# Half of an input projection by a seven-product scheme, in a phase of its own, with its results kept in DRAM

## The chip, the cores and the metric

The kernel runs on one core of one Trainium2 chip. The metric is the time of one execution on the device in microseconds (us), lower is better. The profile comes from one execution that the hardware profiler recorded. TensorE is called PE here, its weight loads PEld, VectorE DVE, ScalarE ACT, GpSimd POOL, and SyncE, which issues all DMAs of this kernel, SP.

## The reference

Two layers work on 1024 tokens of width 1024, float32 throughout. Each layer normalizes its input to h, projects it with one matrix of 1024 x 7764, runs three branches on parts of the result, gates and merges them:

```
p   = split_proj(h @ w_in[l])                    # 7764 columns
ret = rms_norm(retention(ret_q, ret_k, ret_v)) * silu(ret_g)
dsa = dsa_attention(...) * silu(dsa_g)           # top 256 keys per query
gl  = rms_norm(gla(gla_q, gla_k, gla_v, log_a)) * silu(gla_g)
g   = sigmoid(merge)                             # 3 x 1024 columns
y   = (g[0] * (ret @ w_br_ret) + g[1] * (dsa @ w_br_dsa) + g[2] * (gl @ w_br_gla)) @ w_out
x   = x + gate * rms_norm(y, post_norm)
```

## The kernel before

Every dense product is split in three: both operands are kept as a rounded high part and the low rest, and `mm3` (L222) issues high x high, low x high and high x low into the same PSUM bank. h lies transposed in SBUF as `hTh` and `hTl` (128 partitions, 8 blocks of the width, 1024 tokens). A projection comes in two forms. `nat` (L227) puts 128 tokens on the partitions and up to 512 output columns on the free axis, 24 matmuls for a block of tokens; `trans` (L235) puts 128 output columns on the partitions and 512 tokens on the free axis, 24 matmuls as well. Weights are loaded by `wload` or `wide` (L165, L207): one DMA of 256 KB, a cast on ACT for the high part (L176), a subtraction on POOL for the low part (L177). Three raw buffers and ten of each part rotate.

A layer goes in this order: index projection and index scores (`idx_proj`, `idx_scores`, L468 to L509); the retention with its V projection, its q and k projection, a scan over eight blocks and the gate (`ret_gate`, L609), which projects the gate columns, multiplies and transposes; the first GLA projection and scan (`gla_proj` L648, `gla_scan` L694); the merge of the retention (`merge`, L302), which projects 256 gate columns at a time, takes tanh, multiplies them with the branch product and stores the result in DRAM; the second GLA projection and scan, between whose blocks pieces of the conditioning of later norms are put (`cond_part`, L315, twelve in layer 0, four in layer 1); the GLA gates and the DSA gate (`gla_gate` L788, L811 to L818); the transposes of the GLA output and the merge of GLA; the top-k of the index scores (`topk`, L851), 32 rounds of an eight-fold maximum and a replacement for each block of 128 queries; the DSA projections, the attention, and with it the sixteen gate tiles of the DSA merge; the combination of the three branches (L1040 to L1056), the output projection, the norm and the next h.

The order of the instructions on each engine isn't written out: a scheduler lists them by the order of the program and puts later instructions forward where an engine would be idle by its own estimates and buffers are free. So the top-k of blocks 2 to 5 lies on DVE beside the retention and the first scan, and that of blocks 6 and 7 has an explicit edge behind the first product of the GLA merge (L860). Memory is a stack of pools on a left and a right side; a tile can be written when the tiles that lay there before are no longer read. The pools of the second GLA projection lie where the retention's output and the first merge lay.

A scan handles eight blocks of 128 tokens. For two blocks at a time, six levels of exponent tiles are made (L712 to L718: two subtractions on DVE, one exponential on ACT, three products on POOL); for each block then follow a transpose (L737), the state (L747, L753), six score matmuls (L762), seven masked copies on DVE (L763, L768), the output (L774, L778) and its sums of squares.

## Time and profile before

| | us |
|---|---|
| median of 3 runs | 2485.9 (2485.63 to 2487.37) |
| the profiled execution | 2489.89 |
| its span, first to last instruction | 2488.1 |
| busy: PE / PEld / DVE | 2395.1 / 2032.5 / 1704.3 |
| busy: ACT / POOL | 892.9 / 915.0 |

A line of a group of instructions has the line in the kernel, engine, operation, the tile that is written and those that are read, shapes, the count, then busy time and mean duration of one, then the idle time of the engine just before them with what ended it. A matmul's record runs from its issue to its modelled end, and records overlap. A line of stages has the two bounds and the length in us, then for each engine its busy time and count, the granted clock of TensorE as a share of 2.4 GHz, the busy share of the DMA engines and GB/s.

### The profile page before, as it was taken

What the parts mean: (1) busy time and instruction counts of PE and PEld (TensorE: products, weight loads), DVE (VectorE), ACT (ScalarE), POOL (GpSimd) and SP (SyncE); (2) the same over time, 40 slices, a digit from 0 to 9 for tenths busy, and PEclk for the clock granted to TensorE, in tenths of its full rate; (3) what the DMA queues carried; (4) which work ended last, traced back from release to release, by engine and by line L of the source; (5) the groups of instructions that cost most, each with busy time, mean ns of one, the idle gap of its engine ahead of it and who ended that gap; (6) DMA issues with size and microseconds to landing.
All of it is one profiled execution on the core that took longest, in us unless ns stands there. A gap on an engine that the chain in (4) does not pass through costs nothing.

```text
span 2488.1 us, 38048 instructions
## 1 busy us (share of the span) xinstructions
PE 2395.1 (96%) x13680; PEld 2032.5 (82%) x13680; DVE 1704.3 (68%) x3513; ACT 892.9 (36%) x2147; POOL 915.0 (37%) x1304
## 2 busy tenths in 40 slices
PE   8898999999999999999999899999999999999998
PEld 4777788888878998887788677887898789888777
DVE  6599997348749964567567999933554899356652
ACT  4333432232321236663433234222333212566421
POOL 4324344534522352106641244443454225310350
PEclk9999999999999999999999899999999999999999
DMA  8011112224412212007620111222321221210453
GB/s 273 22 35 35 35 41 79 59 87 145 119 60 76 66 48 64 27 22 246 201 90 1 35 35 48 64 61 85 85 63 41 85 85 35 71 41 22 140 199 110
DMA packets 153115, 194.95 MB, mean 78 GB/s; under 512 B 18703, under 2 KB 109147, under 8 KB 152926
## 3 DMA queue, kind: packets, MB, share of 16 engines
q1 hardware_dynamic: 152926, 192.52, 25.4%
q8 instruction: 107, 1.75, 0.3%
q14 instruction: 82, 0.67, 0.1%
HBM read 154.71 MB, written 37.77 MB: 77 GB/s over the span
## 4 chain that ended last, share of the span: by engine, by line
PE 73%; DVE 15%; DMA 4%; issue 3%; POOL 3%; ACT 2%; SPq 0%; DVEq 0%; POOLq 0%; ACTq 0%
PE acc L223 18%; PE acc L224 18%; PE acc L225 18%; DVE mk L855 3%; PE tp L936 2%; DVE m L854 2%; DMA craw<-in_ada_w 2%; PE sc L762 2%; PE o L958 1%; PE sc L921 1%; PE o L955 1%; PE sc L922 1%; PE o L962 1%; PE sc L223 1%; PE sc L224 1%
## 5 line engine op out<-in xcount | busy, mean ns | idle before, releaser
L223 PE MATMUL acc<-whi,hTh 128*128 128x256 f32 (+1 forms) x1600 | 509.8, 319 | 15.5 <-DVE rb L544 8.0
L225 PE MATMUL acc<-whi,hTl 128*128 128x256 f32 (+1 forms) x1600 | 507.4, 317 | 0.0
L224 PE MATMUL acc<-wlo,hTh 128*128 128x256 f32 (+1 forms) x1600 | 506.9, 317 | 0.0
L177 POOL TENSOR_TENSOR wlo<-raw,whi 128x512 fp32r<-128x512 f32 x216 | 283.1, 1318 | 374.8 <-ACT whi L176 343.6
L223 PE MATMUL acc<-hTh,whi 128*128 128x512 f32 x896 | 355.4, 397 | 2.7 <-ACT mt L287 1.8
L224 PE MATMUL acc<-hTl,whi 128*128 128x512 f32 x896 | 353.3, 394 | 0.0
L225 PE MATMUL acc<-hTh,wlo 128*128 128x512 f32 x896 | 352.7, 394 | 0.0
L854 DVE MAX8 m<-mk 128x8 f32<-128x512 f32 (+5 forms) x384 | 341.7, 892 | 8.2
L223 PEld LDWEIGHTS acc<-whi,hTh 128*128 128x128 f32 x1600 | 307.1, 192 | 41.3 <-issue 11.7
L855 DVE MATCH_REPLACE8 mk<-m,mk 128x512 f32<-128x512 f32 (+5 forms) x384 | 336.6, 877 | 0.2
L225 PEld LDWEIGHTS acc<-whi,hTl 128*128 128x128 f32 x1600 | 306.8, 192 | 20.0 <-issue 2.4
L224 PEld LDWEIGHTS acc<-wlo,hTh 128*128 128x128 f32 x1600 | 307.0, 192 | 19.0 <-issue 2.2
L176 ACT CAST whi<-raw 128x512 fp32r<-128x512 f32 x216 | 133.8, 622 | 217.9 <-PE acc L224 139.0
L223 PEld LDWEIGHTS acc<-hTh,whi 128*128 128x128 f32 x896 | 169.0, 189 | 39.9 <-ACT mt L287 2.8
L225 PEld LDWEIGHTS acc<-hTh,wlo 128*128 128x128 f32 x896 | 169.0, 189 | 37.1 <-issue 2.4
L224 PEld LDWEIGHTS acc<-hTl,whi 128*128 128x128 f32 x896 | 169.1, 189 | 34.1 <-issue 1.9
L940 DVE TENSOR_TENSOR ptl<-tp,pth 128x512 fp32r<-128x512 f32 (+1 forms) x160 | 100.6, 635 | 68.6 <-ACT pth L939 59.3
L287 ACT ACTIVATE mt<-acc 128x512 f32<-128x512 f32 x96 | 57.2, 599 | 191.1 <-PE acc L225 136.3
L218 POOL TENSOR_TENSOR wlo<-raw,whi 128x512 fp32r<-128x512 f32 x56 | 76.7, 1378 | 111.2 <-ACT whi L217 110.4
L926 ACT ACTIVATE P<-P,mx 128x256 f32<-128x256 f32 (+7 forms) x128 | 99.8, 781 | 47.0 <-DVE mx L923 46.1
L939 ACT CAST pth<-tp 128x512 fp32r<-128x512 f32 (+1 forms) x160 | 85.7, 545 | 69.5 <-PE o L955 43.3
L973 POOL TENSOR_TENSOR qo<-qo,gt 128x256 f32<-128x256 f32 x32 | 23.5, 735 | 229.4 <-DVE qo L967 208.8
(411 smaller groups left out, 4858.4 us busy)
## 6 DMA issues: line engine op xcount, KB each, us to landing
raw<-in_w_in SPq DMA_DIRECT2D x224, 256.0 KB
yscr<-mu SPq DMA_DIRECT2D x64, 256.0 KB
craw<-in_ada_w SPq DMA_DIRECT2D x64, 256.0 KB
ul<-yscr SPq DMA_DIRECT2D x64, 256.0 KB
aw<-in_ada_w SPq DMA_DIRECT2D x16, 512.0 KB
xt<-in_x SPq DMA_DIRECT2D x16, 512.0 KB
mscr<-mt SPq DMA_DIRECT2D x32, 256.0 KB
ul<-mscr SPq DMA_DIRECT2D x32, 256.0 KB
```

The costliest lines, as they stand in the source:

```text
L176: A.copy(hi[:, :, :off], raw[:, :, :off])
L177: G.tensor_sub(lo[:, :, :off], raw[:, :, :off], hi[:, :, :off].bitcast(FT))
L218: G.tensor_sub(lo, raw, hi.bitcast(FT))
L223: T.matmul(ps, ah, bh, start=start, stop=False)
L224: T.matmul(ps, ah, bl, start=False, stop=False)
L225: T.matmul(ps, al, bh, start=False, stop=stop)
L287: A.activation(t, gp, AF.Tanh, scale=0.5)
L854: V.max(m8, mk[i])
L855: V.match_replace(mk[i], m8, mk[i], TAKEN)
L926: A.activation(P[:, :N], P[:, :N], AF.Exp, scale=-1.0, bias=mx[:, nch - 1:nch], accum_out=den[:, i, n * 4 + g:n * 4 + g + 1])
L939: A.copy(pth[:, :w], tp[:, :w])
L940: V.tensor_sub(ptl[:, :w], tp[:, :w], pth[:, :w].bitcast(FT))
```

## The change

3584 of the 7764 columns (retention gate, GLA q and k, GLA gate, merge gates of the retention and of GLA) are computed in a function of their own, `dense`, right after the index scores, by Strassen's scheme in Winograd's form: the two halves of the 1024 input rows, two blocks of 128 columns and the two halves of the tokens make a 2 x 2 product, for which seven half-size products of 12 matmuls each take the place of eight. Sums of quarters of h (`Th`, `Tl`, four of each) are made once a layer; sums of quarters of the weights are made for each of the 14 groups of 256 columns; partial results are copied out of PSUM and added. All results are transposed (columns on partitions) and go to DRAM: tanh or SiLU already taken for gates. The merges load gate tiles instead of projecting them; the merge of GLA also adds the stored merge of the retention, so that the combination after attention loads one tensor less. The gates of retention and GLA are loaded and multiplied after the transposes of the branch outputs (`to_br`); before, they were multiplied ahead of the transposes. GLA q and k are loaded. The DSA gate is projected as before, but ahead of the new phase. The explicit edge for the top-k is gone. In the combination one sum moves from DVE to POOL.

```diff
+    gts = dram.tile([2, 8, 128, S], FT, name="gts")
+    rgs = dram.tile([4, 128, S], FT, name="rgs")
+    ggs = dram.tile([4, 128, S], FT, name="ggs")
+    qks = dram.tile([4, 128, S], FT, name="qks")
...
+    def to_br(pl, wn, gscr_, brh, brl, kb0, nk, p):
         ps = tpp()
-        for s in range(2):
+        for s in range(nk):
             T.transpose(ps[:, blk(s)], wn[:, blk(s)], ident)
-        pv = ps[:, :256].rearrange("p (k n) -> p k n", k=2)
-        A.copy(brh[:, kb0:kb0 + 2, blk(p)], pv)
-        V.tensor_sub(brl[:, kb0:kb0 + 2, blk(p)], pv, brh[:, kb0:kb0 + 2, blk(p)].bitcast(FT))
+        f = pl.tile([128, nk, 128], FT, tag="bf", bufs=2, name="bf")
+        SY.dma_start(f, gscr_[kb0:kb0 + nk, :, blk(p)].rearrange("k p n -> p k n"))
+        V.tensor_mul(f, f, ps[:, :nk * 128].rearrange("p (k n) -> p k n", k=nk))
+        hi, lo = brh[:, kb0:kb0 + nk, blk(p)], brl[:, kb0:kb0 + nk, blk(p)]
+        A.copy(hi, f)
+        G.tensor_sub(lo, f, hi.bitcast(FT))
...
+    def merge(pl, l, i, wbr, brh, brl, dst, prev=None):
         for dp in range(4):
-            wG = wload(w_in[l], [(C_MG + i * D + dp * 256, 256)])
             wB = wload(wbr[l], [(dp * 256, 256)], nk=4)
-            ts = [gates(pl, wG, cb, hf, nb) for cb in range(2) for hf in range(2)]
             for cb in range(2):
                 for hf in range(2):
+                    at = (dp * 2 + cb, slice(None), slice(hf * 512, (hf + 1) * 512))
+                    t = pl.tile([128, 512], FT, tag="mt", bufs=4, name="mt")
+                    SY.dma_start(t, gts[i][at])
+                    if prev is not None:
+                        u = pl.tile([128, 512], FT, tag="mu", bufs=3, name="mu")
+                        SY.dma_start(u, prev[at])
                     z = branch(wB, cb, hf, brh, brl)
-                    u = pl.tile([128, 512], FT, tag="mu", bufs=2, name="mu")
-                    mm = V.scalar_tensor_tensor(u, ts[cb * 2 + hf], 1.0, z, op0=OP.add, op1=OP.mult)
-                    marks.setdefault(i, mm)
-                    SY.dma_start(dst[dp * 2 + cb, :, hf * 512:(hf + 1) * 512], u)
+                    V.scalar_tensor_tensor(t, t, 1.0, z, op0=OP.add, op1=OP.mult)
+                    if prev is not None:
+                        G.tensor_add(t, t, u)
+                    SY.dma_start(dst[at], t)
+
+    def dense(pz, wl, Th, Tl, groups):
+        k1, k2, t1, t2 = slice(0, 4), slice(4, 8), slice(0, 512), slice(512, 1024)
+        B = {1: (hTh[:, k1, t1], hTl[:, k1, t1]), 2: (hTh[:, k2, t1], hTl[:, k2, t1]),
+             3: (hTh[:, k2, t2], hTl[:, k2, t2]), 4: (Th[3], Tl[3]), 5: (Th[0], Tl[0]), 6: (Th[1], Tl[1]),
+             7: (Th[2], Tl[2])}
+
+        def load(c0, kh, home):
+            if home:
+                a = pz.tile([128, 512], FT, tag="za", bufs=2, name="za")
+            else:
+                a = ring.tile([128, 512], FT, tag="raw", bufs=3, name="raw")
+            SY.dma_start(a.rearrange("p (k n) -> p k n", k=4),
+                         wl[kh * 512:(kh + 1) * 512, c0:c0 + 128].rearrange("(k p) n -> p k n", p=128))
+            return a
+
+        def conv(a):
+            hi = ring.tile([128, 512], FR, tag="whi", bufs=10, name="whi")
+            lo = ring.tile([128, 512], FR, tag="wlo", bufs=10, name="wlo")
+            A.copy(hi, a)
+            G.tensor_sub(lo, a, hi.bitcast(FT))
+            return hi, lo
+
+        def weights(ca, cb):
+            w = {}
+            a11, a21, a22 = load(ca, 0, False), load(cb, 0, True), load(cb, 1, False)
+            w[1] = conv(a11)
+            s_ = pz.tile([128, 512], FT, tag="zt", bufs=2, name="zt")
+            G.tensor_add(s_, a21, a22)
+            w[5] = conv(s_)
+            G.tensor_sub(s_, s_, a11)
+            w[6] = conv(s_)
+            a12 = load(ca, 1, True)
+            w[2] = conv(a12)
+            G.tensor_sub(a21, a11, a21)
+            w[7] = conv(a21)
+            w[4] = conv(a22)
+            G.tensor_sub(a12, a12, s_)
+            w[3] = conv(a12)
+            return w
+
+        def prod(ps, w, n, first):
+            (wh, wl_), (bh, bl) = w[n], B[n]
+            for k in range(4):
+                for j, (a, b) in enumerate(((wh, bh), (wh, bl), (wl_, bh))):
+                    T.matmul(ps, a[:, blk(k)], b[:, k], start=first and k == 0 and j == 0, stop=k == 3 and j == 2,
+                             skip_group_check=not first)
+
+        def snap(ps, sc_):
+            t = pz.tile([128, 512], FT, tag="zs", bufs=6, name="zs")
+            A.activation(t, ps, AF.Copy, scale=sc_)
+            return t
+
+        def plus(t, ps, sc_):
+            if sc_ == 1.0:
+                V.tensor_add(t, t, ps)
+            else:
+                V.scalar_tensor_tensor(t, ps, sc_, t, op0=OP.mult, op1=OP.add)
+
+        def sink(kind, dst, hf, v, inplace=True):
+            if kind == "raw" and inplace:
+                t = v
+            else:
+                t = v if kind == "tanh" and inplace else pz.tile([128, 512], FT, tag="zs", bufs=6, name="zs")
+                if kind == "raw":
+                    A.copy(t, v)
+                else:
+                    A.activation(t, v, AF.Tanh, scale=0.5)
+                    if kind == "silu":
+                        V.scalar_tensor_tensor(t, t, 1.0, v, op0=OP.add, op1=OP.mult)
+            SY.dma_start(dst[:, hf * 512:(hf + 1) * 512], t)
+
+        def tail(w, x_, z_, s2, kind, da, db, sc_):
+            prod(x_, w, 4, False)
+            sink(kind, db, 0, x_, False)
+            prod(z_, w, 3, False)
+            plus(s2, z_, sc_)
+            sink(kind, da, 1, s2)
+
+        late = None
+        for ca, cb, kind, da, db, sc_ in groups:
+            w = weights(ca, cb)
+            x_ = scp()
+            prod(x_, w, 1, True)
+            s1_ = snap(x_, sc_)
+            if late:
+                tail(*late)
+            z_ = tpp()
+            prod(z_, w, 5, True)
+            prod(x_, w, 6, False)
+            s2 = snap(x_, sc_)
+            y_ = acc()
+            prod(y_, w, 2, True)
+            plus(s1_, y_, sc_)
+            sink(kind, da, 0, s1_)
+            prod(x_, w, 7, False)
+            s3 = snap(x_, 1.0)
+            plus(s3, z_, 1.0)
+            sink(kind, db, 1, s3)
+            late = (w, x_, z_, s2, kind, da, db, sc_)
+        tail(*late)
...
+        ptr = pool(f"ptr{l}")
+        pT = pool(f"pT{l}", side="right")
+        Th = [pT.tile([128, 4, 512], FR, name=f"Th{i}") for i in range(3)]
+        Tl = [pT.tile([128, 4, 512], FR, name=f"Tl{i}") for i in range(3)]
...
+        pdg = pool(f"pdg{l}", side="right")
+        for b in range(4):
+            sl = blk(b)
+            f1, f3, f2 = [pdg.tile([128, 4, 128], FT, tag="f", bufs=4, name="f") for _ in range(3)]
+            (h11, l11), (h12, l12), (h22, l22) = hq(0, 0, b), hq(0, 1, b), hq(1, 1, b)
+            G.tensor_sub(f1, h12, h11)
+            G.tensor_sub(f3, h22, h12)
+            G.tensor_add(f1, f1, l12)
+            G.tensor_add(f3, f3, l22)
+            G.tensor_sub(f1, f1, l11)
+            G.tensor_sub(f3, f3, l12)
+            V.tensor_add(f2, f3, h11)
+            V.tensor_add(f2, f2, l11)
+            for i, f in enumerate((f1, f2, f3)):
+                lohi(i, sl, f)
+        for cq in range(2):
+            wg = wload(wl, [(C_DG + cq * 256, 256)])
+            for p in range(NB):
+                ps = nat(wg, p, 256)
+                t = pdg.tile([128, 256], FT, tag="dgt", bufs=2, name="dgt")
+                A.activation(t, ps[:, :256], AF.Tanh, scale=0.5)
+                V.scalar_tensor_tensor(t, t, 1.0, ps[:, :256], op0=OP.add, op1=OP.mult)
+                SY.dma_start(gscr[p, :, cq * 256:(cq + 1) * 256], t)
+        pdg.release()
+        ptr.release()
         pk.release()
-        pki.release()
-
+        pz = pool(f"pz{l}")
+        Th.append(pz.tile([128, 4, 512], FR, name="Th3"))
+        Tl.append(pz.tile([128, 4, 512], FR, name="Tl3"))
+        for b in range(4):
+            sl = blk(b)
+            f4 = pz.tile([128, 512], FT, tag="zs", bufs=6, name="f4").rearrange("p (k n) -> p k n", k=4)
+            h21, l21 = hq(1, 0, b)
+            V.tensor_sub(f4, h21, Th[1][:, :, sl].bitcast(FT))
+            V.tensor_add(f4, f4, l21)
+            V.tensor_sub(f4, f4, Tl[1][:, :, sl].bitcast(FT))
+            lohi(3, sl, f4)
+        groups = [(C_RG + j * 256, C_RG + j * 256 + 128, "silu", rgs[2 * j], rgs[2 * j + 1], 1.0) for j in range(2)]
+        groups += [(C_GQ + j * 128, C_GK + j * 128, "raw", qks[2 * j], qks[2 * j + 1], 0.125) for j in range(2)]
+        for n_, i in enumerate((0, 2)):
+            if i:
+                groups += [(C_GG + j * 256, C_GG + j * 256 + 128, "silu", ggs[2 * j], ggs[2 * j + 1], 1.0)
+                           for j in range(2)]
+            groups += [(C_MG + i * D + j * 256, C_MG + i * D + j * 256 + 128, "tanh", gts[n_][2 * j],
+                        gts[n_][2 * j + 1], 1.0) for j in range(4)]
+        dense(pz, wl, Th, Tl, groups)
+        pz.release()
+        pT.release()
...
+        def ret_gate(p):
+            t = pr.tile([128, 4, 128], FT, tag="ra", bufs=2, name="gt")
+            V.tensor_tensor(out=t, in0=vo[:, p, :].rearrange("p (h n) -> p h n", h=4),
+                            in1=rr[:, p, :, None].to_broadcast([128, 4, 128]), op=OP.mult)
+            to_br(prb, t.rearrange("p h n -> p (h n)"), rgs, brh, brl, 0, 4, p)
...
+            SY.dma_start(kT, qks[2 * g + 1])
+            SY.dma_start(qT, qks[2 * g])
...
+        gla_scan(0, got0)
         pm = pool(f"pm{l}", side="right")
-        merge(pm, l, 0, w_br_ret, brh, brl, yscr[0], 3)
+        merge(pm, l, 0, w_br_ret, brh, brl, yscr[0])
...
+        for p in range(NB):
+            for g in range(2):
+                to_br(pm, (got0, got1)[g][3][:, p, :], ggs, brh, brl, 2 * g, 2, p)
         tap("gla", brh.bitcast(FT))
-        pm = pool(f"pn{l}", side="right")
-        merge(pm, l, 2, w_br_gla, brh, brl, yscr[1])
+        merge(pm, l, 1, w_br_gla, brh, brl, yscr[1], yscr[0])
...
-        for i in range(2, 6):
+        for i in range(2, NB):
             topk(i)
-        with tc.issue_after(marks[2].ins):
-            for i in range(6, NB):
...
+                u, t = us[0][n_ % 4], us[1][n_ % 4]
+                SY.dma_start(t, mscr[d, :, hs])
+                SY.dma_start(u, yscr[1][d, :, hs])
                 n_ += 1
-                t = u[2]
-                (V if n_ % 4 == 0 else G).tensor_add(u[0], u[0], u[1])
                 z = branch(by_k(wB[dp]), cb, 0, *dst[hf], True)
                 V.scalar_tensor_tensor(t, t, 1.0, z, op0=OP.add, op1=OP.mult)
-                V.tensor_add(t, t, u[0])
+                G.tensor_add(t, t, u)
                 A.copy(hTh[:, d, hs], t)
                 V.tensor_sub(hTl[:, d, hs], t, hTh[:, d, hs].bitcast(FT))
         tap("yT", hTh.bitcast(FT))
```

## Rows read from the trace of the kernel before

**Rows 1.** Page, part 1: busy us (share of the span) and instructions of each engine.
```profile
PE 2395.1 (96%) x13680; PEld 2032.5 (82%) x13680; DVE 1704.3 (68%) x3513; ACT 892.9 (36%) x2147; POOL 915.0 (37%) x1304
```

**Rows 2.** Page, part 4: the chain that ended last, by engine.
```profile
PE 73%; DVE 15%; DMA 4%; issue 3%; POOL 3%; ACT 2%; SPq 0%; DVEq 0%; POOLq 0%; ACTq 0%
```

**Rows 3.** Groups by form: busy us, mean ns | idle before; projections of 512 columns.
```profile
L223 PE MATMUL acc<-hTh,whi 128*128 128x512 f32 x896 | 355.4, 397 | 2.7 <-ACT mt L287 1.8 <-ACT qo L893 0.5 <-DVE mu L311 0.4
```

**Rows 4.** Timeline of PE, layers 0 and 1: start us, us, instruction.
```profile
761.87 0.40 PE L223 MATMUL acc<-brh,whi 128*128 128x512 f32 x1
...
772.87 0.40 PE L223 MATMUL acc<-hTh,whi 128*128 128x512 f32 x1
...
1804.98 0.28 PE L223 MATMUL acc<-whi,hTh 128*128 128x256 f32 x1
...
1806.42 0.28 PE L223 MATMUL acc<-whi,hTh 128*128 128x256 f32 x1
```

**Rows 5.** Stages: us, busy (count) of PE, PEld, DVE, ACT, POOL, clock, DMA.
```profile
303.00:515.00 212.00, 209.48 (x1128) 172.01 (x1128) 138.94 (x276) 61.85 (x153) 95.85 (x133) 0.99 0.22 65
515.00:715.00 200.00, 193.21 (x1427) 169.17 (x1425) 126.28 (x309) 61.24 (x173) 88.75 (x126) 0.99 0.36 104
1295.00:1525.00 230.00, 217.71 (x1061) 180.77 (x1062) 206.98 (x482) 79.38 (x215) 69.75 (x105) 0.97 0.11 27
1525.00:1742.00 217.00, 213.28 (x1146) 175.22 (x1145) 133.83 (x266) 62.29 (x153) 94.78 (x132) 0.99 0.23 66
1742.00:1915.00 173.00, 172.27 (x1354) 156.60 (x1353) 91.72 (x230) 60.46 (x171) 85.11 (x125) 1.00 0.24 68
```

**Rows 6.** Timeline, last block of the second scan, layer 0, and what follows.
```profile
706.43 0.27 PE L737 MATMUL tp<-kc,kd 128*128 128x128 f32 x1
...
711.56 0.49 PE L774 MATMUL o<-vo,ats 128*128 128x128 f32 x2 [2.31 <-DVE ats L768]
...
713.97 0.25 ACT L784 COPY vo<-tp 128x128 f32<-128x128 f32 x1
...
716.51 0.63 PE L224 MATMUL acc<-hTl,whi 128*128 128x512 f32 x1
...
716.93 0.63 PE L225 MATMUL acc<-hTh,wlo 128*128 128x512 f32 x1
```

**Rows 7.** Line 737 in the second scan of layer 1, then of layer 0.
```profile
L737 PE MATMUL tp<-kc,kd x8: 272/301/329, 1783.5 to 1898.3; 128*128 128x128 f32 x8
...
L737 PE MATMUL tp<-kc,kd x8: 270/272/275, 562.5 to 706.4; 128*128 128x128 f32 x8
```

**Rows 8.** Timeline of DVE and POOL, head of the first scan, layer 1.
```profile
1529.02 0.67 DVE L622 TENSOR_TENSOR brl<-tp,brh 128x512 fp32r<-128x512 f32 x1
...
1543.26 4.91 DVE L677 TENSOR_TENSOR_SCAN bc<-runs,mab 128x256 f32<-128x256 bf16 x4
...
1562.67 1.17 POOL L718 TENSOR_TENSOR XQ<-e,qT 64x128 f32<-64x128 f32 x2
```

**Rows 9.** Page, part 5: weight conversion and top-k.
```profile
L177 POOL TENSOR_TENSOR wlo<-raw,whi 128x512 fp32r<-128x512 f32 x216 | 283.1, 1318 | 374.8 <-ACT whi L176 343.6
...
L854 DVE MAX8 m<-mk 128x8 f32<-128x512 f32 (+5 forms) x384 | 341.7, 892 | 8.2
...
L855 DVE MATCH_REPLACE8 mk<-m,mk 128x512 f32<-128x512 f32 (+5 forms) x384 | 336.6, 877 | 0.2
...
L176 ACT CAST whi<-raw 128x512 fp32r<-128x512 f32 x216 | 133.8, 622 | 217.9 <-PE acc L224 139.0
```

**Rows 10.** Stages as in rows 5: combination of layer 0, GLA merge of layer 1.
```profile
1132.00:1192.00 60.00, 54.53 (x220) 41.54 (x221) 48.91 (x56) 19.37 (x34) 42.83 (x29) 0.97 0.90 294
1915.00:2045.00 130.00, 128.77 (x577) 104.84 (x576) 106.04 (x156) 28.99 (x56) 30.20 (x24) 1.00 0.25 75
```

**Rows 11.** Groups by form: POOL and DVE sums of the combination.
```profile
L1050 POOL TENSOR_TENSOR ul<-ul,ul 128x512 f32<-128x512 f32 x24 | 37.3, 1558 | 11.6 <-DMA ul<-yscr 11.6
...
L1053 DVE TENSOR_TENSOR ul<-ul,ul 128x512 f32<-128x512 f32 x32 | 36.0, 1126 | 1.5
```

## What the change should do to the time

> **What bounds the kernel now.** I read the busy times first: PE is busy for 96% of the span, DVE for 68%, and the chain that ended last runs through PE for 73% of its length, most of it in the three matmul lines of the split product, L223 to L225 [rows 1, 2]. A busy PE could still be a waiting one, so the next view is the spacing of its matmuls. Their duration of 0.39 us is latency; they start much closer together [rows 3]. From 761.87 to 772.87 us 48 matmuls of 512 columns start: 0.229 us each. From 1804.98 to 1806.42 us twelve of 256 columns start: 0.120 us each, so the narrow form costs 0.240 us per 512 columns [rows 4]. Third, by stage: the stretch from the end of the retention to the end of the second GLA scan has PE busy for 209 of 212 and 193 of 200 us in layer 0, 213 of 217 and 172 of 173 us in layer 1 [rows 5]. The reader should see why: the scans are long chains over ACT, DVE and POOL, and the queue of PE is filled between their steps with projections that depend on nothing there (gates of the first merge, GLA and DSA gates). The kernel is bound by PE nearly everywhere because independent matmuls cover the chains.
>
> **The matmuls saved.** Per layer the columns concerned cost now: retention gate, 8 x 24 = 192 matmuls of 512; GLA q and k, 192; merge gates of two branches, 768; together 1152 x 0.229 = 263.8 us. The GLA gate: 384 of 256, 384 x 0.120 = 46.1 us. Sum 309.9 us. After: 14 groups x 7 products x 12 = 1176 matmuls of 512, at 0.229 us 269.3 us. Saved: 40.6 us a layer, **81 us** in all. That is all that the scheme gives, if PE stays as full as now.
>
> **What the phase of its own takes away from the scans.** This is the term that decides. Out of the stretch of [rows 5] go GLA q and k (44.0 us), the gates of the first merge (16 x 24 x 0.229 = 87.9), the GLA gate (46.1) and the DSA gate (46.1, moved in front of the phase): 224 us of matmuls that fill PE there now. If PE still bounded the stretch it would shrink from 412 to 188 us in layer 0 and from 390 to 166 us in layer 1. Two scans must fit into that, and what they need uncovered can be bounded by rows.
> One block of a scan, bare: the last block of the second scan of layer 0 has no filler in it and takes from its transpose at 706.43 to its last copy at 714.22 us, 7.8 us, during which PE mostly waits (for DVE's masks until 711.56) [rows 6]. One block with filler between its steps: eight first transposes from 1783.5 to 1898.3 us, seven intervals, 16.4 us each; with eight more pieces of the conditioning in between (layer 0) from 562.5 to 706.4, 20.6 us each [rows 7]. The head of a scan, from the last write of the retention (1529.7) to the end of the cumulative sums (1548.2), takes 18.5 us, and its first exponent tiles until 1563.8 us another 15 [rows 8].
> Bare, both heads and 16 blocks are 2 x 33.5 + 16 x 7.8 = 192 us; if the second head hides under the first scan, 174 us. The filler left (V projections, 384 x 0.120 = 46; branch matmuls of the first merge, 192 x 0.229 = 44) partly fits into the heads, and what doesn't delays the blocks: if none fitted, 90 us more, 282 us. I take 212 us, 20 above the bare chain, since the heads have room for more than half of the 90. Against 166 us that is **+46 us** in layer 1 (between +8 and +116). Layer 0 has eight more pieces of conditioning, 7 x 4.2 = 29 us by [rows 7]: 241 against 188 us, **+53 us** (between +1, where half of them hides, and +123). Its parts don't move in the code; they lose their cover.
>
> **Other terms.**
> The Strassen phase itself: per group PE has 84 x 0.229 = 19.2 us, POOL seven low parts and four sums at 1.32 us, 14.5 us, ACT seven casts, three snapshots and four tanh at 0.62 us, 8.7 us [rows 9]. PE alternates between three kinds of PSUM banks, so that each snapshot or sum has at least one product (2.75 us) before its bank is used again. DVE adds three sums of about 0.7 us and, in four groups, SiLU. So it should run on PE; I allow 0.5 us a group, **+7 us** a layer (0 to +14).
> The sums of h for the scheme and the DSA gate lie beside the index scores, where the retention's V projection lies now. That stretch with the retention has PE busy for 218 of 230 us [rows 5]: the retention loses its gate matmuls as cover of its tail (up to +10 us), the index scores get a cover that does not run out (up to -10). I take 0.
> The second merge (GLA) keeps 44 us of matmuls, but reads a gate tile and the first merge's sum and writes one tile per 2.75 us, 0.79 MB: with 2.1 MB of weights 14.7 MB. The fastest stretch for that kind of transfers moved 294 GB/s [rows 10]; that makes 50 us, less some 2 us of loads that can come ahead; they stand in SP's queue behind those for the transposes of the GLA output. Now the merge with its gates takes 130 us [rows 10], so at PE's pace 42 us would be left: **+6 us** a layer (0 to +15).
> The combination after attention loses a third load, and two DVE sums go to POOL or vanish. That stretch has PE busy for only 54.5 of 60 us, with the two-input sums of L1053 at 1.13 us on DVE [rows 10, 11]: **-6 us** a layer (0 to -8).
> The top-k (342 + 337 us on DVE over both layers [rows 9]) loses its order behind the GLA merge. Through the index scores and the Strassen phase, some 340 us, DVE has about 115 us of other work (an estimate at 0.7 us an operation: index scores 35, sums of h 31, DSA gate 7, the phase 42), so of 340 us of top-k a layer some 220 fit; the rest falls into retention and scans, as it does now. **+4 us** a layer (-5 to +20).
> Sum: -81 + 46 + 53 + 14 + 0 + 12 - 12 + 8 = **+40 us**. The profiled execution took 2489.9 us (span 2488.1); the median of the runs is 4.0 below it. So 2489.9 + 40 - 4 = 2526, rounded **2525 us**.
>
> **Two rules of the Trainium skill against the trace.** The trace shows interleaving at work: the same scan takes 16.4 us a block with PE full, 7.8 us with PE waiting [rows 6, 7]. "Perfetto Trace Analysis", section Optimization Strategy, says that a kernel whose most contended engine changes over time may gain by interleaving those regimes; this change takes them apart. By that rule the sign is that of my forecast; without it only the saved matmuls would count, 2405 us.
> After the bare block the matmuls of 512 columns start 0.42 us apart instead of 0.229, at the lower level of the granted clock [rows 6]; nothing but a few us of sparse work had gone before. "TensorE: Matmul & The Clock Gate", section What's actually happening, says that the halved clock is the default and that activity lifts it. An uncovered scan would then run its own matmuls at half pace: about 3 us more in a block, some 10 bare blocks a layer, up to 60 us in all, as far as they lie on the chain. I count it in the upper end, not in the sum.
>
> **Rivals.**
> *The saving comes through (faster).* The scheduler starts the second GLA projection under the first scan, as soon as the first merge has freed its memory, and the fillers sit in gaps where they delay nothing. Then the stretch costs +8 and +1 us, the other terms stand at their lower halves: -81 + 9 + 7 + 6 - 14 = -73 for both layers, 2413 us; with a quarter of the 90 us of filler in the way in each layer, 2458. I price it at **2440 us**. For it: the bare block is 7.8 us in the trace. Against it: in the trace the second projection begins only when the first merge is through. It decides from the stretch of layer 1: under about 205 us (166 + 40) this case wins.
> *The cover is lost, by about what is saved (no change).* The stretch costs +35 to +45 us a layer, without the other terms: **2486 us**.
> *POOL becomes the bound of the phase (slower still).* If its eleven operations a group collide with DVE on their inputs, 1.56 us as in L1050 [rows 11], and wait seven times for casts of 0.6 us, a group takes 17.2 + 4.2 = 21.4 us against 19.2: 28 x 2.2 = +62 us on the forecast, **2587 us**. Against it: most of DVE's work in that phase is top-k and sums out of PSUM, and L177 keeps 1.32 us beside top-k now.
>
> **Chances and range.** Forecast 0.50 (own range 2500 to 2575), saving comes through 0.35, no change 0.08, POOL 0.07. The range leaves out the lower third of the second case and the upper end of the last: **2425 to 2585**. A measurement of this kernel can tell about 0.2% (5 us): faster 0.35, within 0.08, slower 0.57.
>
> **What would show it.** Right: in the Strassen phase PE starts a matmul every 0.229 us and the phase takes 270 to 285 us a layer; from its end to the GLA merge PE shows gaps before L762 and L774 of the old numbering, the granted clock falls in the second scan, and the stretch of two scans takes over 205 us. Wrong: the stretch takes 170 to 190 us (then the second case), or the phase takes over 300 us with PE waiting for low parts of the weights (then POOL), or PE waits in the phase for snapshots that stand behind top-k.

## The result and the profile after

The changed kernel takes **2790.3 us** (2789.39 to 2795.71, four runs) against 2486.2 for the kernel before (2485.63 to 2487.37, four runs): ratio 1.1227, 95% interval 1.1207 to 1.1246. The forecast was 2525, the range 2425 to 2585. The sign was right; the loss of 304 us is over seven times the 40 of the sum. The profiled execution has a span of 2789.2 us.

The page of the changed kernel: busy time by engine, then two of the rows of forty slices (PE's busy tenths and the granted clock in tenths).

```profile
PE 2454.6 (88%) x12960; PEld 2030.1 (73%) x12960; DVE 1785.8 (64%) x3533; ACT 994.7 (36%) x2319; POOL 1333.4 (48%) x1636
...
PE   6889999978665699999998899999695668999998
...
PEclk8899999998665799999999999999895659999999
```

PE executes 720 matmuls fewer, as it should, and yet its busy time rises by 60 us against [rows 1], in a span 301 us longer. A busy time counts records at the lower clock at their longer duration, so it hides the saving. The two hollows in both rows are the GLA scans, one stretch in each layer. The chain that ended last ran through PE for 73% [rows 2]; now:

```profile
PE 37%; DVE 6%; POOL 3%; DMA 2%; issue 2%; ACT 1%; SPq 0%; DVEq 0%; POOLq 0%; ACTq 0%
```

By stage, with columns as in [rows 5]: the seven-product phase, the retention's scan, the two GLA scans, the transposes of the GLA output and the GLA merge of layer 0; then the two scans of layer 1.

```profile
183.00:478.00 295.00, 288.18 (x1231) 232.45 (x1231) 279.80 (x476) 113.86 (x202) 210.03 (x160) 0.99 0.37 108
526.00:615.00 89.00, 75.78 (x410) 59.74 (x408) 85.84 (x148) 31.93 (x116) 37.91 (x40) 1.00 0.14 42
615.00:782.00 167.00, 123.75 (x670) 97.75 (x671) 83.73 (x188) 40.60 (x121) 74.73 (x118) 0.75 0.28 89
782.00:923.00 141.00, 85.87 (x426) 56.84 (x424) 93.96 (x238) 34.31 (x111) 61.37 (x104) 0.61 0.32 98
923.00:943.00 20.00, 11.84 (x42) 7.76 (x42) 5.68 (x12) 4.11 (x11) 8.13 (x12) 0.61 0.19 53
943.00:1003.00 60.00, 49.76 (x232) 40.31 (x231) 12.78 (x22) 8.04 (x18) 33.39 (x30) 0.91 0.67 216
...
1986.00:2150.00 164.00, 122.86 (x670) 97.32 (x671) 81.93 (x186) 40.16 (x118) 73.75 (x117) 0.77 0.29 90
2150.00:2277.00 127.00, 81.00 (x411) 57.83 (x410) 60.87 (x163) 34.30 (x111) 59.00 (x105) 0.61 0.14 42
```

Where the scans of [rows 5] had PE busy for 97 to 100% at a granted clock of 0.99 or 1.00 (of 2.4 GHz), they now have it busy for 74 and 61% at 0.75 and 0.61, and no other engine is full in its place: DVE has 50 to 67%, POOL 44 to 45%. That is a chain without cover. The phase itself has PE busy for 288 of 295 us.

The boundaries of the table are the last copy of the retention's scan, the last copy of the second GLA scan and the last product of the GLA merge in each trace (layer 0 counted from the span's start):

| stretch, us | before, layers 0 and 1 | after | change | forecast |
|---|---|---|---|---|
| to the end of the retention | 292.5, 218.2 | 615.5, 537.4 | +323, +319 | +278 |
| the two GLA scans | 421.7, 401.4 | 307.6, 291.3 | -114, -110 | -171, -178 |
| transposes and GLA merge | 125.2, 130.7 | 79.5, 79.4 | -46, -51 | -82 |
| rest of the layer | 455.9, 442.5 | 445.6, 432.9 | -10, -10 | -2 |

The forecast of the first row is the phase (269 + 7) and the DSA gate (46) less the retention's gate (44). The three rows above the last miss by 45 and 41, 57 and 68, 36 and 31 us: together 278 us in the direction of slower. The prediction drew the first border later: its stretch of the scans begins at 303 and 1525 us [rows 5], about where the retention's gate ends, 10.5 and 11.5 us after the border of the table. By its own border the retention misses by some 35 and 30 us and the scans by 67 and 79.

### The profile page after: what moved, and what is told of

Its sections match the earlier page's. It is cut to its first block, busy times and chain, and to the rows that moved or that the text cites. A ratio compares the mean times of both kernels' runs of the same rounds, so it can differ in the third digit from the quotient of the medians.

```text
span 2789.2 us, 37962 instructions
## 1 busy us (share of the span) xinstructions
PE 2454.6 (88%) x12960; PEld 2030.1 (73%) x12960; DVE 1785.8 (64%) x3533; ACT 994.7 (36%) x2319; POOL 1333.4 (48%) x1636
## 4 chain that ended last, share of the span: by engine, by line
PE 37%; DVE 6%; POOL 3%; DMA 2%; issue 2%; ACT 1%; SPq 0%; DVEq 0%; POOLq 0%; ACTq 0%
PE acc L227 6%; PE acc L228 6%; PE acc L229 6%; PE sc L368 5%; PE tp L368 3%; PE acc L368 1%; PE sc L909 1%; PE tp L1067 1%; DVE mk L989 1%; PE sc L229 1%; PE sc L228 1%; PE sc L227 1%; DVE ats L915 1%; DMA craw<-in_ada_w 1%; PE o L1089 1%
## 5 line engine op out<-in xcount | busy, mean ns | idle before, releaser
L227 PE MATMUL acc<-whi,hTh 128*128 128x256 f32 (+1 forms) x1216 | 386.6, 320 | 47.8 <-ACT vo L838 40.6
L229 PE MATMUL acc<-whi,hTl 128*128 128x256 f32 (+1 forms) x1216 | 388.7, 320 | 0.0
L228 PE MATMUL acc<-wlo,hTh 128*128 128x256 f32 (+1 forms) x1216 | 386.0, 317 | 0.0
L181 POOL TENSOR_TENSOR wlo<-raw,whi 128x512 fp32r<-128x512 f32 x120 | 157.9, 1328 | 84.6 <-ACT whi L180 76.1
L368 PE MATMUL sc<-Th,whi 128*128 128x512 f32 x336 | 134.2, 399 | 3.6 <-DVE f L675 3.6
L368 PE MATMUL sc<-Th,wlo 128*128 128x512 f32 x336 | 133.9, 398 | 0.8 <-POOL wlo L343 0.8
L368 PE MATMUL sc<-Tl,whi 128*128 128x512 f32 x336 | 133.2, 397 | 0.0
L343 POOL TENSOR_TENSOR wlo<-za,whi 128x512 fp32r<-128x512 f32 x84 | 110.7, 1332 | 0.0
L227 PE MATMUL acc<-brh,whi 128*128 128x512 f32 x256 | 103.9, 413 | 5.5 <-ACT brh L288 4.7
L228 PE MATMUL acc<-brl,whi 128*128 128x512 f32 x256 | 103.2, 403 | 0.0
```

What stands on the lines that cost most here:

```text
L181: G.tensor_sub(lo[:, :, :off], raw[:, :, :off], hi[:, :, :off].bitcast(FT))
L227: T.matmul(ps, ah, bh, start=start, stop=False)
L228: T.matmul(ps, ah, bl, start=False, stop=False)
L229: T.matmul(ps, al, bh, start=False, stop=stop)
L343: G.tensor_sub(lo, a, hi.bitcast(FT))
L368: T.matmul(ps, a[:, blk(k)], b[:, k], start=first and k == 0 and j == 0, stop=k == 3 and j == 2, skip_group_check=not first)
```

## The experiments

Each is the changed kernel with an edit, unless it says otherwise, and is compared with its 2790.3 us. Each but the last was run once, in a later session; the kernel before took 2484 to 2488 us there, and the four runs of the changed kernel lie 6.3 us apart, so that a difference of a few us shows nothing by itself. Stage times are from each kernel's own trace; "layer 1" is counted from the end of layer 0.

### Cover given back: the gates of the first merge

```diff
-        merge(pm, l, 0, w_br_ret, brh, brl, yscr[0])
+        merge_own(pm, l, 0, w_br_ret, brh, brl, yscr[0])   # the merge of before, gates projected in it
-            groups += [(C_MG + i * D + j * 256, ...) for j in range(4)]
+            if i:
+                groups += [(C_MG + i * D + j * 256, ...) for j in range(4)]
```

> The changed kernel, but the gates of the retention's merge are projected in the merge again, as in the kernel before (four groups of fourteen leave the phase; 11 us of matmuls more a layer). Theory 'cover': the phase loses 4 x 19.2 = 77 us a layer, and the 88 us of matmuls lie under the first scan and the second projection, where PE waits: that stretch grows by 15 to 30 us only. In all 90 to 125 us less, 2665 to 2700. Rival 'work': the matmuls cost their time wherever they lie: 22 us more, about 2812.

Measured: 2748.3 us, 42 less, between the two. The retention ends 75 us sooner in each layer, as 4 groups of 19 us should give. But the two scans grow from 307.6 to 363.1 us and from 291.3 to 342.7: of 88 us of matmuls a layer 55 and 51 cost time, some 40% hide.

### Cover given back: GLA q and k, GLA gate, DSA gate

```diff
-            SY.dma_start(kT, qks[2 * g + 1])
-            SY.dma_start(qT, qks[2 * g])
+            wq = wload(wl, [(C_GQ + g * 128, 128), (C_GK + g * 128, 128)])
+            ...  # trans and scaled copies, as before
...
         gla_scan(1, got1, ...)
+        ...  # eight GLA gate tiles to ggs, then the DSA gate as it stood before
```

> The changed kernel, but GLA q and k are projected in the GLA projection, and the GLA gate and the DSA gate are projected after the second scan in program order, where they can be pulled under it, as before the change (the GLA gate still goes to DRAM and is applied on the transposed side; ten groups stay in the phase). Theory 'cover': the phase loses 4 x 19.2 = 77 us a layer and the place beside the index scores up to 46; 134 us of matmuls return to the scans, whose stretch grows by 20 to 60 us. In all 100 to 170 us less, 2620 to 2690. Rival 'work': the matmuls cost their time wherever they lie: 22 us more, about 2812.

Measured: 2734.3 us, 56 less, again between. 134 us of matmuls a layer return; the scans grow by 68 and 58 us. About half hides.

### Both together

> The edits of the two kernels that bring cover back taken together: the gates of the first merge, GLA q and k, the GLA gate and the DSA gate are projected where they were before the change; six groups (retention gate, gates of the GLA merge) stay in the phase. Alone the one gave 42 us, the other 56. Theory 'additive' (each matmul that returns is half hidden): 42 + 56 = 98 us less, about 2692. Theory 'whole cover' (with all fillers back the scans are bound by PE again and everything that returns is hidden to the measure it was before): the phase falls to 115 us, both scans take 400 to 425 us again as before, the scheme still saves 16.5 us a layer, the GLA merge and the retention lose some 20 us a layer against before: 2490 to 2560.

Measured: 2681.5 us, 109 less: additive. The scans take 429 and 404 us again, and PE is busy for 94 and 89% of them in place of 74 and 61%, as the view by stage of this kernel shows (layer 0):

```profile
450.00:690.00 240.00, 226.74 (x1200) 183.82 (x1200) 201.54 (x342) 67.30 (x169) 103.82 (x142) 0.97 0.23 69
690.00:880.00 190.00, 169.06 (x1048) 138.38 (x1048) 119.35 (x269) 53.97 (x150) 84.58 (x121) 0.87 0.37 114
```

So what the scans of before hid can be read off: 222 us of matmuls for 121 and 113 us of time. Yet this kernel, with six groups left in the phase, is still 195 us slower than the one before. Its retention ends 158 us later than before in layer 0, of which six groups less the retention's gate are worth 72. The phase splits index scores and retention, which lay beside each other (in the kernel before the retention's first transposes come at 162.3 us, ahead of the end of the last index score at 189.7; here at 352.8, after 166.3). With the DSA gate back in its old place, nothing is left to cover the scores: from 110 to 165 us of layer 0 the retention's V projection kept PE busy in the kernel before (first two lines), and in this kernel PE waits while DVE is full (last two).

```profile
110.00:138.00 28.00, 28.00 (x133) 23.14 (x132) 26.50 (x70) 9.09 (x19) 0.00 (x0) 1.00 0.00 1
138.00:165.00 27.00, 27.00 (x127) 22.46 (x127) 25.93 (x58) 9.73 (x20) 13.79 (x12) 1.00 0.30 78
...
110.00:138.00 28.00, 12.37 (x28) 6.76 (x28) 28.00 (x40) 10.11 (x21) 17.47 (x12) 0.50 0.00 0
138.00:165.00 27.00, 16.89 (x33) 8.52 (x33) 27.00 (x45) 11.10 (x21) 11.31 (x8) 0.50 0.08 19
```

PE is idle there for 26 us, a part of the 86 us by which the retention's end is later than the six groups explain.

### The same phase with ordinary products

```diff
-        def snap(ps, sc_): ...
-        ...  # the seven products and their sums
+        for ca, cb, kind, da, db, sc_ in groups:
+            w = wload(wl, [(ca, 256)] if cb == ca + 128 else [(ca, 128), (cb, 128)])
+            for c_, dst in ((0, da), (1, db)):
+                for hf in range(2):
+                    sink(kind, dst, hf, trans(w, c_, hf), sc_ if c_ == 0 else 1.0)
```

> The changed kernel with the phase in the same place and the same results kept in DRAM, but each of its 14 groups as eight ordinary products (four sums of 24 matmuls) in place of seven; the sums of h for the scheme are still made. Theory 'order': the phase runs at PE's pace either way, so the scheme is worth its 14 x 12 x 0.229 = 38.5 us a layer, and this kernel takes 65 to 80 us more than the changed one, 2855 to 2870; then the change loses some 380 us by its order and wins 77 back by the scheme. Rival 'side work': the scheme's snapshots and sums on ACT, DVE and POOL delay others by as much as it saves; then this kernel stays within 25 us of the changed one, 2765 to 2815.

Measured: 2833.2 us, 43 more: neither. From the end of the index scores in the changed kernel (182.5 us) to the retention's first transposes it takes 376 us against 343, 33 more, which is 1344 matmuls at 0.227 against 1176 at 0.231; at the end of the layer 23 and 19 us are left. A part is given back beside PE: with fewer sums on DVE the top-k ends 49 and 51 us sooner, and the retention takes 86.5 and 83.8 us in place of 89.6 and 89.8. So seven products in place of eight are worth 43 us in this order. But this kernel still makes the sums of h that only the scheme needs, and without them the changed kernel takes 30 us less (below). By subtraction the scheme is worth some 13 us net, and of the 347 us by which this kernel is slower than the one before, about 317 belong to the new order with its results in DRAM; no run has ordinary products without the sums. The order, not the scheme, is the loss.

### The clock of an uncovered scan

A block of the second scan of layer 1, PE's instructions (start, us, instruction, idle time before it and what ended it):

```profile
2242.89 0.47 PE L884 MATMUL tp<-kc,kd 128*128 128x128 f32 x1
2243.81 0.70 PE L894 MATMUL sc<-vo,kn 64*64 64x128 f32 x8 [0.45 <-ACT kn L886]
2245.94 0.59 PE L906 MATMUL sc<-kc,qk 128*128 128x2 f32 x2 [1.43 <-DVE st L900]
2246.39 2.91 PE L909 MATMUL sc<-XQ,XK 128*128 128x128 f32 x12
2252.79 0.74 PE L921 MATMUL o<-vo,ats 128*128 128x128 f32 x2 [3.49 <-DVE ats L915]
2253.46 0.69 PE L925 MATMUL o<-st,qe 64*64 64x128 f32 x4
2254.08 0.80 PE L921 MATMUL tp<-vo,ats 128*128 128x128 f32 x2
2254.81 0.69 PE L925 MATMUL tp<-st,qe 64*64 64x128 f32 x4
2255.43 0.47 PE L884 MATMUL tp<-kc,kd 128*128 128x128 f32 x1
```

12.5 us from transpose to transpose, where [rows 6] had 7.8 from the transpose to the last copy: the chain's own matmuls run mostly at the lower of the clock's two levels, 1.2 GHz (granted on average 0.59 of 2.4 GHz from 2182 to 2277 us; 2.9 us for the scores, 1.6 in the block of [rows 6]), and PE waits 3.5 us for DVE's masked copies in place of the 2.3 of [rows 6], because the next pair's exponent tiles stand between the copies on DVE.

A first kernel was to put idle matmuls into the gaps; as run it had ten in each of the 32 blocks, and in 26 of these all ten came ahead of the last score product, in the chain, instead of behind it:

> The changed kernel with 14 idle matmuls (128 x 512) put into each of the last five blocks of the first GLA scan and all eight of the second: 4 behind the state products, 10 behind the score products, into a bank that nobody reads. They add work and take none away. In the changed kernel a block of the second scan of layer 1 takes 11.8 us from transpose to transpose (2182.6 to 2266.3, seven intervals), its score matmuls 2.9 us instead of 1.6, at a low granted clock; PE's own steps in it sum to some 8 us, at full clock some 4.4. Theory 'clock': the added matmuls keep the granted clock up, a block falls to 8 to 9 us, 26 such blocks win about 3 us each: 50 to 80 us less in all, 2710 to 2740. Rival 'chain': the steps of DVE, ACT and POOL set the pace, the clock doesn't matter; then 14 matmuls at 0.229 to 0.42 us just fill the waits or lengthen them: 0 to 60 us more, 2790 to 2850.

Measured: 2841.7 us, 51 more, in the rival's range; but ten matmuls of 0.23 us or more stood in the way of most blocks, so it does not decide about the clock. The second put them where PE waits:

```diff
+                    if g == 1:
+                        idle(mms, 4)    # four 128 x 512 matmuls, behind all state products
...
+                    if g == 1:
+                        idle(mms, 10)   # ten, behind all six score products
```

> The changed kernel with idle matmuls (128 x 512, nobody reads the result) in the eight blocks of the second GLA scan of each layer alone: 4 behind the state products, 10 behind the last score product, where PE waits for DVE. They add work and take none away. In the changed kernel these eight blocks take 108.4 us in layer 0 (first transpose 814.7, last copy 923.1) and 94.3 in layer 1 (2182.6 to 2276.9). Theory 'clock': PE's own steps in a block, some 8 us at the low granted clock, fall to some 4.4, a block gets 2.5 to 3.3 us shorter: 40 to 53 us less in all, 2737 to 2750. Rival 'chain': DVE, ACT and POOL set the pace; the extra matmuls are hidden or lengthen the blocks: 0 to 40 us more, 2790 to 2830.

Measured: 2770.1 us, 20 less: the clock counts, at half or less of what was expected. Ten of the 20 lie in the eight blocks of the second scan of layer 1 and three in the transposes and the merge behind it; the rest lies outside the edited stretch and is of the size of the spread between runs. The first transposes of the eight blocks of layer 1, of the changed kernel and then of this one (duration; first and last start):

```profile
L884 PE MATMUL tp<-kc,kd x8: 272/473/476, 2182.6 to 2266.3; 128*128 128x128 f32 x8
```

```profile
L884 PE MATMUL tp<-kc,kd x8: 270/329/477, 2180.2 to 2255.6; 128*128 128x128 f32 x8
```

Over seven intervals that is 12.0 and 10.8 us a block; the granted clock of the stretch went from 0.59 (2182 to 2277 us) to 0.86 (2180 to 2264 us). The last block, with no next pair to prepare, can be compared in three kernels, from its transpose to its last copy: before (layer 0, [rows 6]), changed, and with idle matmuls (both layer 1).

```profile
706.40:714.30 7.90, 5.03 (x35) 3.23 (x33) 2.84 (x8) 1.51 (x8) 0.15 (x1) 0.91 0.01 2
...
2266.30:2276.90 10.60, 7.79 (x35) 5.36 (x33) 3.19 (x10) 1.74 (x10) 0.99 (x3) 0.50 0.08 25
...
2255.60:2264.30 8.70, 7.78 (x49) 5.63 (x47) 3.46 (x10) 1.74 (x10) 0.98 (x3) 1.00 0.09 30
```

So the clock is worth 1 to 2 of the 4 us between 7.8 and 12.0; the preparation of the next pair is most of the rest (10.8 against 8.7 with the clock up). In layer 0, where pieces of the conditioning lie between the blocks, nothing is won (14.0 and 14.2 us a block).

### One set of exponent tiles

```diff
+                XK, XQ = sets[qq % 2 if g else 0]     # a second pair of tiles, in p1
```

> The changed kernel with a second set of the exponent-product tiles (XK, XQ) for the second scan, so that the tiles of the next pair of blocks needn't wait for the score matmuls of this pair. In the changed kernel a pair of blocks of the second scan of layer 1 takes 23.7 us (2182.6 to 2207.7 to 2230.7 to 2255.4, first transposes), 11 of them the six levels of tiles between the scores of one pair and those of the next (2196.6 to 2207.6). Theory 'one set': the tiles are made beside the blocks, a pair falls by 4 to 7 us, three intervals a scan: 12 to 20 us in layer 1 and up to as much in layer 0, 2755 to 2778. Rival 'engines': POOL (some 15 us of products and square roots a pair) and DVE set the pace of a pair and the new order delays the block's own steps: within 8 us of the changed kernel.

Measured: 2788.3 us, the rival: no change. A block that waits for no tile (2213.5 to 2225.5 us) takes 12.0 us at the low clock. Then both edits at once:

> The changed kernel with both edits that alone gave little in the second scan: a second set of exponent-product tiles, and the idle matmuls (4 behind the state products, 10 behind the scores of a block). Alone, the second set leaves a block that waits for no tile at 12.0 us at the low granted clock (2213.5 to 2225.5), and the idle matmuls leave 10.8 us a block, since eleven us of tiles lie between the scores of two pairs. Theory 'two limits, one behind the other': without both, a block of layer 1 falls to 8 to 9.5 us, the eight blocks from 94.3 to 66 to 78, some 16 to 28 us less there and 5 to 20 in layer 0, where the pieces of the conditioning lie between: 2740 to 2770. Rival 'engines': DVE and POOL in order of their queues set 10 to 11 us a block whatever the tiles and the clock: 2765 to 2785.

Measured: 2781.8 us, in the rival's range. The first transposes of layer 1 with both:

```profile
L885 PE MATMUL tp<-kc,kd x8: 272/328/476, 2178.7 to 2256.8; 128*128 128x128 f32 x8
```

11.2 us a block on average: 9.8 in the last five (2207.6 to 2256.8), but 15.4 and 13.5 in the first two, where exponent tiles and weight conversions stand between the block's own steps on DVE and POOL. No single cause sets the 12 us: an uncovered block is a chain through four engines, and taking away the wait for tiles, the low clock or both gave 0, 1.2 and 0.8 us a block.

### The second head

```diff
-                ps = scp()
+                ps = (acc if g else scp)()      # both places in gla_proj
```

> The changed kernel, with the four banks that the second GLA projection takes for its transposes and its small product taken from the rotation of the projections in place of that of the scores. In the changed kernel the second head begins only when the first scan is over (782.5, first block of the second scan at 814.7), though the first merge, whose memory it needs, ended at 709 (2075 in layer 1). Theory 'banks': score banks rotate in program order, so the head waited for the last scores of the first scan; freed from that, it lies under the first scan and 20 to 35 us a layer go: 2720 to 2750. Rival 'engines': DVE's cumulative sums and the V projection then stand ahead of the steps of the first scan and delay them by as much: within 15 us of the changed kernel, 2775 to 2805.

Measured: 2752.5 us, 38 less: theory 'banks', if 2.5 us above its range. First transposes of the second projection of layer 0, changed kernel, then this one:

```profile
L802 PE MATMUL sc<-kc,ga x8: 372/418/418, 778.2 to 782.4; 128*16 128x128 f32 x8
```

```profile
L802 PE MATMUL acc<-kc,ga x8: 270/273/273, 708.5 to 709.2; 128*16 128x128 f32 x8
```

The head begins 70 us sooner, at the end of the first merge, and the two scans together take 14 us less in layer 0 and 19 in layer 1. So the second head did not start as soon as its memory was free, as the first rival of the prediction had it, because of a rotation of PSUM banks: the banks are given out in program order, and the head's came behind those of the last block. That alone did not defeat the rival: with the head freed the stretch of layer 1 still takes 273 us, far over its limit of 205.

### The GLA merge's loads

> The changed kernel, with eight buffers each in place of four and three for the gate tiles and the stored sums that the GLA merge loads. From its first to its last product that merge takes 60 us in the changed kernel (943 to 1003) for 44 us of matmuls. Theory 'late loads': the loads wait for buffers; they come earlier, 8 to 14 us a layer go: 2762 to 2775. Rival 'transfers' (the DMA engines or POOL's additions set the pace): within 6 us of the changed kernel.

Measured: 2784.0 us, 6 less, the rival by its number, and no more than runs of one kernel differ. From first to last product the merge went from 60.3 to 54.2 us in layer 0 and from 59.7 to 54.2 in layer 1, but in layer 0 it began 5 us later, and the rest of each layer takes 3 us more. In the changed kernel its products wait for more than PE (943 to 1003 us, DVE: busy, mean ns, idle before and by whom):

```profile
L319 DVE SCALAR_TENSOR_TENSOR mt<-mt,acc 128x512 f32<-128x512 f32 x15 | 10.2, 687 | 36.6 <-PE acc L229 17.5 <-DMA mt<-gts 15.4 <-POOL mt L321 3.7
L286 DVE TENSOR_TENSOR bf<-bf,tp 128x256 f32<-128x256 f32 x6 | 2.5, 420 | 10.5 <-DMA bf<-ggs 10.5
```

### The sums of h beside the index scores

```diff
-            G.tensor_sub(f1, h12, h11)
-            ...  # six sums on POOL and two on DVE for each block
-            for i, f in enumerate((f1, f2, f3)):
+            for i, f in enumerate((h11, h12, h22)):
```

> The changed kernel without the sums of quarters of h for the seven products: three quarters of h themselves are split in their place (the casts on ACT and the low parts on DVE stay; 24 sums on POOL and eight on DVE a layer are left out, and the results of the phase are not those of the reference). Beside those sums DVE's two-input steps of the index scores take 1.29 us (110 to 138 us) against 0.68 in the kernel before, and the phase begins when the scores end. Theory 'sums slow the scores': the phase begins 10 to 20 us sooner in each layer: 2750 to 2770. Rival 'top-k': DVE, busy all the time either way, fills what is left with top-k, and the scores end as late: within 8 us of the changed kernel.

Measured: 2760.1 us, 30 less, as theory 'sums slow the scores' says: the phase begins 12.0 and 12.7 us sooner. DVE's weighted sums of the index scores, 86 to 184 us, of the changed kernel and of this one:

```profile
L614 DVE SCALAR_TENSOR_TENSOR mk<-tr,wts,mk 128x512 f32<-128x512 f32 x17 | 15.9, 939 | 0.0
```

```profile
L614 DVE SCALAR_TENSOR_TENSOR mk<-tr,wts,mk 128x512 f32<-128x512 f32 x18 | 13.8, 770 | 0.5 <-ACT tr L611 0.5
```

These DVE operations, which read two operands from SBUF, take longer beside POOL's sums; but 17 times 0.17 us is only 3 of the 12 us. Most of the rest is probably the sums' own work on DVE (eight of them take 9.7 us), in a stretch where DVE has next to no idle time and the phase waits for the last score; the run takes both away at once.

### The order of the top-k

```diff
-        for i in range(2, NB):
-            topk(i)
+        with tc.issue_after(begun.ins):          # first product of the phase
+            for i in range(2, 6): topk(i)
+        with tc.issue_after(marks[l, 1].ins):    # first product of the GLA merge
+            for i in range(6, NB): topk(i)
```

> The changed kernel with the top-k ordered by hand: blocks 2 to 5 behind the first product of the seven-product phase, blocks 6 and 7 behind the first product of the GLA merge (in the changed kernel all of it may come forward, and it runs from 117 to 625 us in layer 0). Theory 'DVE ahead of the phase': before the phase (138 to 183 us) DVE is busy 45 of 45 us, with index scores, sums of h and top-k; the phase begins when the last score is written; without top-k there it begins 12 to 20 us sooner a layer, and the retention after it, 89 us with DVE busy 91, gets 8 to 15 us shorter. In all 35 to 65 us less, 2725 to 2755. Rival 'no change': the scores are slow by themselves, DVE's top-k only fills gaps, and what the retention wins the attention loses by waiting for the masks: within 12 us, 2778 to 2802.

Measured: 2861.3 us, 71 more, which neither expected. The first edge held nothing back (it orders the scheduler's list, and the top-k starts at 118 us as before). The second did: the top-k ends at 1115 us in layer 0 in place of 625. The retention gains 6 us, and the stretch from the end of the DSA queries to the combination takes 271.5 us in place of 227: in the trace DVE runs rounds of the last block's top-k until 1115 us, while the DSA queries were done at 1063. So an edge like the old one costs more than it gives in the changed kernel: the merge behind whose first product that top-k begins is shorter there, and is over 119 us before the top-k ends (71 in the kernel before).

The same order in the kernel with all cover back, with the freed head and the larger buffers:

> The kernel with all cover back (six groups in the phase, 2681.5 us), with the second head freed from the score banks, the top-k ordered by hand and eight buffers in the GLA merge. With cover the scans are bound by PE, so the freed head gives less there than the 38 us alone. Theory 'barrier': what is left over the kernel before sits ahead of the retention's end, where the phase splits index scores and retention, which lay beside each other (that end comes 158 us later than before, in layer 0, of which the six groups are worth 72); the top-k order gives part of that back: 2600 to 2645. Rival 'scans': the rest sits in the scans and the merge: below 2560.

Measured: 2750.2 us, 69 more than the kernel with the cover back and outside both ranges. The scans take 21 and 13 us less, but from the GLA merge to the end of the layer it takes 54 and 51 us more: the late top-k outweighs the rest, so it says nothing of the barrier.

### One part alone, in the kernel before

```diff
# in the GLA merge of before
+                    SY.dma_start(r_, prev[at])
                     V.scalar_tensor_tensor(u, ts[cb * 2 + hf], 1.0, z, op0=OP.add, op1=OP.mult)
+                    G.tensor_add(u, u, r_)
# in the combination
-                (V if n_ % 4 == 0 else G).tensor_add(u[0], u[0], u[1])
-                V.tensor_add(t, t, u[0])
+                G.tensor_add(t, t, u)
```

> The kernel before with one part of the change alone: the merge of GLA adds the stored merge of the retention (a load and a sum on POOL for each of 16 tiles), so that the combination after the attention loads two tensors in place of three and its sum runs on POOL. The combination fell from 50.0 to 44.7 us in layer 0 and from 52.7 to 44.5 in layer 1 with the change. Theory 'the combination's gain stands alone': in the merge PE sets the pace (128.8 of 130 us), so its extra load and sum are hidden: 8 to 14 us less than before, 2472 to 2478. Rival 'it is paid back in the merge': within 4 us of the kernel before.

Measured: **2475.2 us** (2471.99 to 2478.06, five runs) against 2488.1 for the kernel before in the same session (nine runs): ratio 0.9952, interval 0.9939 to 0.9966. It beats both kernels, and it is the part of the change that puts work under PE's cover instead of taking it out: from first to last product the GLA merge takes 106.0 and 107.4 us (106.0 in both layers before), and the combination falls from 50.0 to 45.6 and from 52.7 to 41.3 us.

## Why the prediction was wrong

**Right.** What bounds the kernel, and that the scans' loss of cover decides. The matmuls saved: 33 of 40.6 us a layer show in the phase. The phase at PE's pace: 1176 products at 0.231 us are 272 us, and 55 matmuls of the retention's V projection fill in as well, 13 us; the rest of 295.7 is 11 us of gaps. POOL did not become its bound. The combination: -5 and -8 us for -6. The falling clock in the second scan and gaps ahead of the scores and outputs were announced.

**The scans: the term was mis-sized.** Against 212 us (layer 1) and 241 us (layer 0) stand 291 and 308, 79 and 67 more. The step that failed is "Bare, both heads and 16 blocks are 2 x 33.5 + 16 x 7.8", with the 20 us on top of it. The row behind the 7.8 [rows 6] is the last block of a scan, beside which no tiles for a next pair are prepared, and it ran its matmuls at the full clock that the covered blocks before it had kept up. In layer 1 the eight blocks of the second scan take 94.3 us, 11.8 each, and the five uncovered blocks of the first 61.7, 12.3 each: 55 of the 79 us. The heads came out as forecast, 69 us for 67. Another 23 us are the three blocks before those five, where the branch matmuls of the first merge did not fit into the heads. These blocks and the five after them, layer 1:

```profile
2022.00:2088.70 66.70, 64.99 (x368) 53.03 (x367) 32.27 (x70) 12.02 (x37) 27.37 (x37) 1.00 0.57 181
2088.70:2150.40 61.70, 37.15 (x181) 26.14 (x179) 30.01 (x81) 12.58 (x53) 27.30 (x53) 0.56 0.09 27
```

The three blocks take 43 us more than 3 x 7.8, where the sum had 20 us for all the filler that was left.

**The clock stood in the wrong place.** The prediction saw [rows 6] fall to the lower level and put up to 60 us into the upper end, "not in the sum". Idle matmuls in the second scans alone won at most 20 us net of their own time, and the last block of a scan takes 1.9 us less with the clock up. As a price it was of the right order; as a tail it was wrong, since the same missing cover makes the long blocks and the low clock: they come together.

**Ahead of the retention's end: "I take 0" was wrong**, by 45 and 41 us, or 35 and 30 by the prediction's own border. It let the gain under the scores offset the loss at the retention's tail. Both were losses: 12 us a layer go with the sums of h; the phase has 11 us of gaps for the 7 allowed; the retention's scan, without gate matmuls, takes 89 us with PE busy for 76. Some 10 us are not accounted for. That scores and retention no longer overlap is read from the order of the trace and from the kernel with the cover back, and no run takes the barrier alone away.

**The GLA merge: +6 was +42 and +37.** The 130 us of [rows 10] include 25 us of transposes and first steps ahead of the first product (1914.9 to 1939.7 us), which the gates' matmuls covered (PE busy for 128.8). These steps lie uncovered now (923 to 943 us, PE busy 11.8 of 20) and had no time of their own in the sum. The merge itself takes 60, for 50 less 2 forecast. Transfers were bounded at 294 GB/s, the rate of another stretch; 216 were reached here, with DMA waits in front of DVE.

**The top-k: +4 was about right by luck,** for another reason than given: by the run with the top-k ordered by hand it costs the retention 6 us.

The wrong terms of the scans and of the merge have one root. The fillers were removed from the sum at their full 224 us in the scans and 88 in the merge, and what they had covered was then priced too low: by its shortest example in the scans, at nothing ahead of the merge's first product. The measured exchange is that 222 us of fillers cost 113 to 121 us inside the scans; taken out, they win only that, while they cost 19.4 us a group in the phase. "Perfetto Trace Analysis" of the Trainium skill, section Optimization Strategy, from which the prediction took that interleaving regimes may help, agrees with this case: half of the interleaved work was free.

## What to carry to other kernels

Work that hides under a latency chain is worth only the time by which its removal shortens that stretch (here half of its own), so a cheaper form of it must save more than the hidden half, or stay in its place. Price a bare chain by a block from its middle, with the preparation of the next one beside it and at the clock that a waiting PE gets, never by its last block. Look also for work beside the one that moves: here the index scores and the retention lay beside each other, and a phase put between them parted them. An edit that adds small work under a full engine and takes it off an uncovered stretch, as the stored merge did (0.5%), was the safer one here.

## What the runs showed of the hardware

Fourteen idle matmuls of 512 columns a block, 3.2 us at full speed, kept the mean granted clock of the second scan of layer 1 at 0.86 in place of 0.59 and shortened its eight blocks by 10 us, though they are pure extra work. "TensorE: Matmul & The Clock Gate" of the Trainium skill, section What's actually happening, has the throttled state as the default and activity as what releases it; these two clocks agree.

A weighted sum of the index scores on DVE, two operands in SBUF, took 1.29 us on average from 110 to 138 us, with POOL busy for 23 of 28 us, where the same step takes 0.68 us in the kernel before with POOL idle (all widths); over the whole stretch 128 x 512 takes 0.94 against 0.77 without those sums. "SBUF — State Buffer" of the Trainium skill, section Who interferes with whom, names the port pair that DVE and GpSimd share as the one contention between engines; the runs here agree for operations with two inputs in SBUF.

In the phase a matmul of 512 columns starts every 0.2325 us on average where its moving operand lies in the tiles of the sums of h and every 0.229 us where it is h itself. A group passes from the one to the other:

```profile
219.75 0.40 PE L368 MATMUL sc<-Th,wlo 128*128 128x512 f32 x1
...
221.15 0.40 PE L368 MATMUL sc<-Th,wlo 128*128 128x512 f32 x1
221.39 0.39 PE L368 MATMUL acc<-hTh,whi 128*128 128x512 f32 x1
...
223.90 0.39 PE L368 MATMUL acc<-hTh,wlo 128*128 128x512 f32 x1
```

Here six intervals take 1.40 us in the first and eleven take 2.51 us in the second. The kernel whose tiles hold plain quarters of h in place of the sums shows the same two averages, so it goes with the tiles and not with what is in them; why is open.
